# Encoder block on one core: stores issued later in SyncE's order, a head's steps drawn closer, the last low part ahead of evictions

## The chip, the core and the metric

The kernel runs on one core of a Trainium2 chip. Its engines work side by side, each through its own instructions in program order: TensorE (PE in the profile) multiplies, VectorE (DVE) and ScalarE (ACT) do elementwise work, SyncE (SP) issues nearly all DMA transfers, and GpSimd (POOL) issues the transfers that add to what is already in SBUF. An instruction that waits holds up everything behind it on its engine. The metric is device time in microseconds, as the median of repeated runs.

## What is computed

One encoder block with two branches, for 256 tokens of width 2048, in float32:

```python
xn = rms_norm(x, norm_pre_w[l])
z = xn @ w_in[l]
u_lru, g_lru, q, k, v, g_attn, m_lru, m_attn = jnp.split(z, split_at, axis=-1)
u = centred_depthwise_conv(u_lru, conv_w[l], conv_b[l])
h = rg_lru(u, ..., False) + rg_lru(u, ..., True)
y_a = h.astype(x.dtype) * jax.nn.silu(g_lru)
q = partial_rope(q.reshape(bsz, s, N_HEADS, HEAD_DIM), cos, sin)
k = partial_rope(k.reshape(bsz, s, N_KV_HEADS, HEAD_DIM), cos, sin)
y_b = windowed_gqa(q, k, v, attn_sink[l]) * jax.nn.silu(g_attn)
merged = (jax.nn.sigmoid(m_lru) * (y_a @ w_proj_a[l])
          + jax.nn.sigmoid(m_attn) * (y_b @ w_proj_b[l]))
x = x + rms_norm(merged @ w_out[l], norm_post_w[l])
```

There are 16 heads of width 128 in 4 groups; `w_in` has 13312 columns, the other three matrices 2048.

## The kernel before

**Two parts of each number.** Products are made with operands of a rounded type (fp32r). To keep float32 precision each operand is split into a high part (a cast, on ACT) and a low part (the rest, a subtraction on DVE), and three products are added: high by high, high by low and low by high. `lag_parts` (L120) issues such a cast at once and the subtraction one half step later.

**Steps and half steps.** The weights come in 182 loads of 1 MB. Each is a step: the load into one of three raw buffers, the cast into `wh` by `ahead` (L974), the subtraction into `wl` by `low` (L966), and the products with it. A step has two half steps, hs = 2i and 2i + 1. In the loop at the end of `body` (L991 to L1009), at half step 2i SP is given the load of step i + 3; then whatever has been put down for this half step is issued in the order in which it was put down; then, on even half steps, the cast of step i + 2; at last the products of the half step on PE. `at(hs, fn)` (L138) puts work down for a half step, `soon(fn, d)` (L147) for d half steps after the present one, and `early(hs, fn)` (L144) ahead of all other work of a half step. So half steps set each engine's order; when things run is up to the semaphores. A half step on PE is twelve wide products, or six in the saving scheme below.

**Steps that save products.** Some blocks are multiplied two by two with seven products instead of eight (`add_seven`, L587). Its weights are sums of blocks: a step of this kind adds its load to weights that are already in a "chain" buffer, by an accumulating DMA that POOL issues once the low part of the step before it in the chain is done. Its left sides are differences of activations (`sums`, L652), also split into parts.

**What goes to DRAM and back.** SBUF has 29 large buffers (`unit`). What isn't needed for long is stored and taken back later: the parts of four differences (xee1 to xee4, high and low), the sigmoids of the merge gates (tm0 to tm2, sm2 and sm3), and the gated output of the LRU branch in four pieces (ya0 to ya3). `put_away` (L124) issues such a store on SP, 0.5 MB each. A store on SP waits for the engine that makes its data, and the loads behind it wait with it. Merge gates and differences are stored four half steps after they are complete (L561, L670), ya two half steps after the gating that completes it: `lru_pair` (L444) gates 20 half steps after its base b, and L871 puts the store at b + 22.

**A head.** `head` (L753) puts the steps of one attention head down behind its base: `scores` (PE), `expo` (DVE: scale, mask, maximum), `powers` (ACT: exponential and sum), `normalise` (DVE and ACT: `p` times the reciprocal), `flip` (PE: transposes of `p` into `pt`), `p_parts` (ACT: `ph`, and one half step later DVE: `pl`), `values` (PE: product with v into `o`), `gate_out` (DVE: `o` times the gate). Heads start three half steps apart. There is one buffer for `ph` and one for `pl`, so a head's `ph` can be written only after the `values` of the head before.

**The end.** The last steps multiply by `w_out`; `take_o` (L928) evicts each block: squares and their sum on ACT, times the norm's weight on DVE. The last step is made for the first 128 tokens and then for the others, so that the first half's output can be finished beside the second half's products.

Of the kernel before, what the change touches and what calls it, by code (L numbers as in the profile page):

```python
# [27 lines left out]
EPS = 1e-6  # L28
UNITS = 29
CHAIN = 2  # L30
DECAY = 10
SPIN = 10
G = 1
LRU0 = 14
LRU_PACE = 22
# [47 lines left out]
def body(ctx, tc, x, xT, wall, wlru, pvec, npost, ident_d, mask_d, rope_d, out):  # L83
    nc = tc.nc
    const = ctx.enter_context(tc.tile_pool(name="const", bufs=1))
    units = ctx.enter_context(tc.tile_pool(name="units", bufs=UNITS))
    chain = ctx.enter_context(tc.tile_pool(name="chain", bufs=CHAIN))
    ring = ctx.enter_context(tc.tile_pool(name="ring", bufs=3))
# [5 lines left out]
    def unit(name, dt=F32, shape=(P, 4, S)):  # L94
        return units.tile(list(shape), dt, tag="u", name=name)

    def bank(name, shape=(P, 2, S)):
        return psum.tile(list(shape), F32, tag="bg", name=name, bufs=4)
# [4 lines left out]
    def half_unit(name, tag, dt=F32, bufs=2):  # L103
        return small.tile([P, 2, S], dt, tag=tag, name=name, bufs=bufs)
# [5 lines left out]
    def tiny(name, n=2):  # L110
        return small.tile([P, n], F32, tag="tiny", name=name, bufs=24)
# [8 lines left out]
    def lag_parts(h, l, src):  # L120
        nc.scalar.copy(h, src)  # L121
        soon(lambda: nc.vector.tensor_tensor(l, src, h.bitcast(F32), ALU.subtract))

    def put_away(name, t):  # L124
        d = away.tile(list(t.shape), F32, tag=name, name=f"{name}_away")
        nc.sync.dma_start(d, t.bitcast(F32))
        return d
# [7 lines left out]
    steps, due = [], {}  # L135
    now = [0]

    def at(hs, fn):  # L138
        assert hs >= now[0], (hs, now[0])
        due.setdefault(hs, []).append(fn)  # L140
# [6 lines left out]
    def soon(fn, d=1):  # L147
        at(now[0] + d, fn)
# [8 lines left out]
    def parts_tiles(i):  # L157
        highs[i], lows[i] = (ring.tile([P, 2048], F32R, tag=f"w{s}", name=f"w{s}{i}", bufs=3) for s in "hl")
# [18 lines left out]
    def pieces(i):  # L177
        if isinstance(raws[i], list):
            return [(slice(h * 1024, (h + 1) * 1024), t) for h, t in enumerate(raws[i])]
        return [(slice(0, 2048), raws[i])]  # L180
# [7 lines left out]
    def mm3(ps, wh, wl, xh, xl, start, stop):  # L188
        nc.tensor.matmul(ps, wh, xh, start=start, stop=False)
        nc.tensor.matmul(ps, wh, xl, start=False, stop=False)  # L190
        nc.tensor.matmul(ps, wl, xh, start=False, stop=stop)  # L191
# [232 lines left out]
    for i, fn in enumerate([  # L424
# [12 lines left out]
    ]):  # L437
        at(DECAY + i // 2, fn)


    sgl, sga = [], []
    ya, yb = [None] * 8, [None] * 8
# [109 lines left out]
    def gate_take(units_of, c, t, ps, scale=1.0):  # L552
        if c not in units_of:
            units_of[c] = unit(f"mg{c}", F32, (P, 2, 512))
        nc.scalar.activation(units_of[c][:, t], ps, AF.Sigmoid, scale=scale)
        if c in ((0, 1) if units_of is sm else (3,)):
            return
        name = "sm" if units_of is sm else "tm"
        written[name, c] = written.get((name, c), 0) + 1
        if written[name, c] == 2:  # L560
            soon(lambda: gone.update({(name, c): put_away(f"{name}{c}", units_of.pop(c))}), 4)  # L561

    gone, written = {}, {}

# [87 lines left out]
    def sums(name, y, keep=None):  # L652


        fm = lambda r, c, n: y[2 * c + n][:, :, r * P:(r + 1) * P]
        eight = lambda u: u.rearrange("p a (b c) -> p (a b) c", c=P)
        e, out = {}, {}

        def less(d, a, b):
            e[d] = e[b] if isinstance(b, str) else eight(unit(f"{name}{d}"))  # L660
            for n in range(2):
                f = [e[o][:, 4 * n:4 * n + 4] if isinstance(o, str) else fm(*o, n) for o in (a, b)]
                nc.vector.tensor_tensor(e[d][:, 4 * n:4 * n + 4], *f, ALU.subtract)

        def split_of(d):
            h, l = (unit(f"{name}{d}{s}", F32R, (P, 8, P)) for s in "hl")
            lag_parts(h, l, e[d])
            out[d] = (h, l)
            if keep is not None:
                soon(lambda: keep.update({d: [put_away(f"{name}{d}{s}", a) for a, s in ((h, "h"), (l, "l"))]}), 4)  # L670

        def when(hs, gap=2):
            for (d, a, b), n in zip((("e1", (1, 0), (1, 1)), ("e2", (0, 0), "e1"), ("e4", (0, 1), "e2"), ("e3", (1, 0), (0, 0))), hs):
                at(n, lambda d=d, a=a, b=b: less(d, a, b))
                at(n + gap, lambda d=d: split_of(d))
            at(hs[2] + 4, lambda: [e.pop(d) for d in ("e1", "e2", "e4")])
            at(hs[3] + 4, lambda: e.pop("e3"))

        return out, when
# [73 lines left out]
    def head(hd, qh, ql, b):  # L753
        g, j = hd // 4, hd % 4
        sk = pv[:, PV_SINK + hd:PV_SINK + hd + 1]
        ts = [slice(t * P, (t + 1) * P) for t in range(2)]
        v = {}

        def scores():
            v["sc"] = bank(f"sc{hd}")  # L760
            for t in range(2):
                mm3(v["sc"][:, t], qh[:, j, ts[t]], ql[:, j, ts[t]], kv["kh"][:, g], kv["kl"][:, g], True, True)

        def expo():
            p = v["p"] = half_unit(f"p{hd}", "p")
            sc = v.pop("sc")
            m, nm, es = tiny(f"m{hd}"), tiny(f"nm{hd}"), tiny(f"es{hd}")
            dn = v["dn"] = tiny(f"dn{hd}")
            for t in range(2):
                nc.vector.tensor_tensor_reduce(p[:, t], sc[:, t], mask[:, t], P ** -0.5, sk, ALU.add, ALU.max, m[:, t:t + 1])  # L770
            nc.vector.tensor_scalar(nm, m, -1.0, None, ALU.mult)
            v["nm"], v["es"] = nm, es

        def powers():
            p, nm, es, dn = v["p"], v["nm"], v["es"], v["dn"]
            for t in range(2):
                nc.scalar.activation(p[:, t], p[:, t], AF.Exp, bias=nm[:, t:t + 1], accum_out=dn[:, t:t + 1])
            nc.scalar.activation(es, nm, AF.Exp, bias=sk)

        def normalise():  # L780
            dn, rd = v["dn"], tiny(f"rd{hd}")
            nc.vector.tensor_tensor(dn, dn, v["es"], ALU.add)
            nc.vector.reciprocal(rd, dn)  # L783
            for t in range(2):
                nc.scalar.activation(v["p"][:, t], v["p"][:, t], AF.Copy, scale=rd[:, t:t + 1])  # L785

        def flip():
            v["pt"] = bank(f"pt{hd}")
            for kt in range(2):
                for t in range(2):  # L790
                    nc.tensor.transpose(v["pt"][:, kt, ts[t]], v["p"][:, t, ts[kt]], ident)

        def p_parts():
            v["h"] = half_unit(f"ph{hd}", "ph", F32R, 1)
            v["l"] = half_unit(f"pl{hd}", "pl", F32R, 1)
            lag_parts(v["h"], v["l"], v.pop("pt"))

        def values():
            v["o"] = bank(f"o{hd}")
            ks = slice(g * P, (g + 1) * P)  # L800
            for kt in range(2):
                mm3(v["o"][:, 0], kv["vh"][:, kt, ks], kv["vl"][:, kt, ks], v["h"][:, kt], v["l"][:, kt], kt == 0, kt == 1)

        def gate_out():
            y = sga[g][:, j]
            nc.vector.tensor_tensor(y, v["o"][:, 0], y, ALU.mult)
            v.clear()

        for d, fn in ((0, scores), (1, expo), (2, powers), (3, normalise), (6, flip), (7, p_parts), (10, values), (11, gate_out)):
            at(b + d, fn)  # L810

    ended = []
# [1 line left out]
    def heads(g):  # L814
        def then(h, l):
            b = max(now[0] + HEAD0, ended[-1] if ended else 0)
            for j in range(4):
                head(4 * g + j, h, l, b + HEADS_PACE * j)
            ended.append(b + 4 * HEADS_PACE)
        return then  # L820
# [47 lines left out]
        return pairs, when, chunk  # L868

    for c in range(4):  # L870
        at(LRU0 + LRU_PACE * (2 * c + 1) + 22, lambda c=c: gone.update({("ya", c): put_away(f"ya{c}", sgl[c])}))  # L871
    for i in range(4):
        plain += add_heads(f"q{i}", Q0 + i * 512, heads(i))
    plain += add_rows("ml3_", "w_in", ML0 + 3 * 512, xn, gate_evac(tm, 3))
# [91 lines left out]
    def low(i):  # L966
        for sl, t in pieces(i):
            nc.vector.tensor_tensor(lows[i][:, sl], t, highs[i][:, sl].bitcast(F32), ALU.subtract)  # L968
        if i in grow:
            n = grow[i]  # L970
            raws[n] = raws[i]
            nc.gpsimd.dma_start(raws[n], wall[rows_of[steps[n][0]]], accum_op=ALU.add)  # L972

    def ahead(i):  # L974
        if i < len(steps):
            parts_tiles(i)
            for sl, t in pieces(i):
                nc.scalar.copy(highs[i][:, sl], t)  # L978
            soon(lambda: low(i))

    tail = {}
    for i, (row, _, key) in enumerate(steps):
# [95 lines left out]
```

## Time and profile before

| what | value |
|---|---|
| median of 3 runs | 889.18 us (889.05 to 891.41) |
| the profiled execution | 895.12 us |
| its span | 893.3 us |
| granted TensorE clock, mean | 0.997 |
| DMA | 227.74 MB, mean 255 GB/s |
| stores to DRAM that the change moves | 17 of 0.5 MB |

The profile is of one execution. A row of the order of time has the start in us, the duration, the engine, the line in the kernel, the operation, output<-inputs and how many were merged; in brackets stands how long the engine idled before it and what ended that. A row of who waited for whom has the waiting engine, the one waited for, the total in us, the number of waits and the longest. A row of stretches has, behind its bounds, the busy time of PE, PE's weight loads, DVE, ACT and POOL, the granted clock as a share of full speed, the share of the DMA engines that was busy, and GB/s. `raw`, `chain`, `wh` and `wl` are the weights as loaded and their two parts. Numbers behind a name are left out in the rows, so that which step or head a row belongs to follows from its place in the engine's order.

### The profile page before, as it was taken

Reading aid. Unit: us, or ns where it says so; the run is one execution under the profiler, and the core shown is the slowest. Engines: PE = TensorE matmul, PEld = TensorE weight load, DVE = VectorE, ACT = ScalarE, POOL = GpSimd, SP = SyncE. Lnnn points to the kernel's source line nnn. Section 1 sums busy time; section 2 is a strip of 40 time slices with the busy share of each in tenths; the row PEclk is TensorE's granted clock in tenths of the full one; section 3 lists DMA queues with packets and bytes.
Section 4 is the critical chain, followed back from the end, with each engine's and each line's share of the span. In section 5 each row is a group of like instructions: output and inputs, shape, how many; then the busy total and the mean of one; then the engine's idle time right before and its main releaser. Section 6 shows DMA issues by size and latency. Waiting matters only on the chain.

```text
span 893.3 us, 11502 instructions
## 1 busy us (share of the span) xinstructions
PE 878.9 (98%) x4518; PEld 751.3 (84%) x4518; DVE 688.1 (77%) x740; ACT 622.0 (70%) x737; POOL 37.2 (4%) x49
## 2 busy tenths in 40 slices
PE   9999999999999999998999999999999999999996
PEld 9888888888888888886888888887888888888885
DVE  5987976979878695957968667777897767758786
ACT  6977659787777878748695766678966554546653
POOL 0000000000000000100000000000000000100000
PEclk9999999999999999999999999999999999999999
DMA  8756678878979887798699879836866986998893
GB/s 320 277 182 216 234 302 205 324 296 248 275 184 338 230 346 288 204 290 211 255 264 350 294 205 257 231 146 248 208 251 236 272 240 195 318 288 323 223 276 149
DMA packets 38934, 227.74 MB, mean 255 GB/s; under 512 B 4320, under 2 KB 5216, under 8 KB 16224
## 3 DMA queue, kind: packets, MB, share of 16 engines
q1 hardware_dynamic: 32400, 184.43, 54.9%
q0 software_dynamic: 6048, 41.95, 24.3%
q8 instruction: 35, 0.57, 0.2%
q10 hardware_dynamic: 432, 0.63, 0.2%
q14 instruction: 19, 0.16, 0.1%
HBM read 215.98 MB, written 11.01 MB: 254 GB/s over the span
## 4 chain that ended last, share of the span: by engine, by line
PE 83%; ACT 6%; DVE 5%; DMA 4%; issue 1%; SPq 0%; DVEq 0%; ACTq 0%
PE u L208 5%; PE ga L208 5%; PE gl L208 5%; DMA raw<-wall_dram 3%; DVE wl L968 3%; PE gl L210 3%; PE ga L210 3%; PE u L210 3%; PE q__4412 L239 2%; PE pa__5458 L239 2%; PE q__4814 L239 2%; PE v__622 L239 2%; PE ml L239 2%; PE pa__5824 L239 2%; PE q__3915 L239 2%; PE o__6841 L239 2%
## 5 line engine op out<-in xcount | busy, mean ns | idle before, releaser
L968 DVE TENSOR_TENSOR wl<-raw,wh 128x2048 fp32r<-128x2048 f32 x118 | 269.5, 2287 | 75.2 <-ACT wh L978 75.0
L978 ACT CAST wh<-raw 128x2048 fp32r<-128x2048 f32 x118 | 224.9, 1911 | 74.3 <-DMA raw<-wall_dram 23.8
L968 DVE TENSOR_TENSOR wl<-chain,wh 128x2048 fp32r<-128x2048 f32 x56 | 128.0, 2288 | 37.4 <-ACT wh L978 37.4
L978 ACT CAST wh<-chain 128x2048 fp32r<-128x2048 f32 x56 | 107.0, 1913 | 40.1 <-PE pb__6243 L239 7.4
L972 POOL DMA_DIRECT2D chain<-wall_dram x38 | 33.3, 876 | 781.2 <-DVE wl L968 625.8
L208 PE MATMUL ga<-xn,wh 128*128 128x512 f32 x256 | 62.8, 390 | 0.0
L208 PE MATMUL gl<-xn,wh 128*128 128x512 f32 x256 | 62.6, 390 | 0.0
L208 PEld LDWEIGHTS gl<-xn,wh 128*128 128x128 f32 x256 | 47.7, 188 | 9.1
L208 PEld LDWEIGHTS ga<-xn,wh 128*128 128x128 f32 x256 | 47.7, 188 | 9.1
L208 PE MATMUL u<-xn,wh 128*128 128x512 f32 x192 | 47.6, 391 | 0.0
L208 PEld LDWEIGHTS u<-xn,wh 128*128 128x128 f32 x192 | 35.5, 188 | 6.5
L210 PEld LDWEIGHTS ga<-xn,wl 128*128 128x128 f32 x256 | 32.8, 191 | 1.3
L210 PEld LDWEIGHTS gl<-xn,wl 128*128 128x128 f32 x256 | 32.8, 191 | 1.3
L210 PE MATMUL gl<-xn,wl 128*128 128x256 f32 x256 | 33.2, 283 | 0.0
L210 PE MATMUL ga<-xn,wl 128*128 128x256 f32 x256 | 33.2, 283 | 0.0
L210 PEld LDWEIGHTS u<-xn,wl 128*128 128x128 f32 x192 | 24.6, 191 | 1.0
L210 PE MATMUL u<-xn,wl 128*128 128x256 f32 x192 | 24.9, 283 | 0.0
L785 ACT ACTIVATE p<-p,rd 128x256 f32<-128x256 f32 x32 | 14.5, 503 | 14.6 <-DVE rd L783 14.6
L121 ACT CAST ph<-pt 128x512 fp32r<-128x512 f32 x16 | 9.3, 584 | 21.9 <-PE o L191 21.8
L469 DVE SCALAR_TENSOR_TENSOR up<-up,pv 128x255 f32<-128x255 f32 (+1 forms) x48 | 22.5, 481 | 1.1
L770 DVE CUSTOM_DVE_ANT_0 p<-sc,mask,pv 128x256 f32<-128x256 f32 x32 | 14.2, 479 | 7.5 <-PE sc L191 7.4
L398 PE MATMUL u_ps<-xs,wh 128*128 128x256 f32 x128 | 19.0, 291 | 0.5 <-ACT wh L114 0.5
(525 smaller groups left out, 1942.1 us busy)
## 6 DMA issues: line engine op xcount, KB each, us to landing
raw<-wall_dram SPq DMA_DIRECT2D x121, 1024.0 KB, 6.3
chain<-wall_dram POOLq DMA_DIRECT2D x38, 1024.0 KB, 9.3
chain<-wall_dram SPq DMA_DIRECT2D x18, 1024.0 KB, 6.1
lraw<-wlru_dram SPq DMA_DIRECT2D x8, 512.0 KB, 6.0
raw<-wall_dram SPq DMA_DIRECT2D x4, 512.0 KB, 7.3
ya_away<-sg SPq DMA_DIRECT2D x4, 512.0 KB, 6.8
yb<-ya_away SPq DMA_DIRECT2D x4, 512.0 KB, 9.2
pair<-wall_dram SPq DMA_DIRECT2D x4, 512.0 KB, 12.2
```

The source lines that it names most:

```text
L121: nc.scalar.copy(h, src)
L208: nc.tensor.matmul(ps, wh[:, sl], a, start=k == 0, stop=k == KT - 1)
L210: nc.tensor.matmul(ps[:, 1], wl[:, sl], a[:, 0], start=False, stop=False)
L239: nc.tensor.matmul(got[t], a[:, m], w[:, j * 512:(j + 1) * 512], start=k == 0 and m == 0 and not low, stop=low and k == KT - 1)
L398: nc.tensor.matmul(ups[b // 2][:, b % 2, 0], w[:, sl], a[:, m], start=k == 0 and n == 0, stop=k == KT - 1 and n == 2)
L469: nc.vector.scalar_tensor_tensor(u[:, a:b], up[:, a + tap - 2:b + tap - 2], cw[:, tap:tap + 1], u[:, a:b], ALU.mult, ALU.add)
L770: nc.vector.tensor_tensor_reduce(p[:, t], sc[:, t], mask[:, t], P ** -0.5, sk, ALU.add, ALU.max, m[:, t:t + 1])
L785: nc.scalar.activation(v["p"][:, t], v["p"][:, t], AF.Copy, scale=rd[:, t:t + 1])
L968: nc.vector.tensor_tensor(lows[i][:, sl], t, highs[i][:, sl].bitcast(F32), ALU.subtract)
L972: nc.gpsimd.dma_start(raws[n], wall[rows_of[steps[n][0]]], accum_op=ALU.add)
L978: nc.scalar.copy(highs[i][:, sl], t)
```

## The change

The constant AWAY is 8, where the two delays of stores were 4. The store of ya goes from b + 22 to b + 27. In a head the flip and what follows comes one or two half steps earlier. The low part of the last step is put ahead of the other work of its half step; for all other steps `at` does what `soon` did.

```diff
+AWAY = 8
...
-            soon(lambda: gone.update({(name, c): put_away(f"{name}{c}", units_of.pop(c))}), 4)
+            soon(lambda: gone.update({(name, c): put_away(f"{name}{c}", units_of.pop(c))}), AWAY)
...
-                soon(lambda: keep.update({d: [put_away(f"{name}{d}{s}", a) for a, s in ((h, "h"), (l, "l"))]}), 4)
+                soon(lambda: keep.update({d: [put_away(f"{name}{d}{s}", a) for a, s in ((h, "h"), (l, "l"))]}), AWAY)
...
-        for d, fn in ((0, scores), (1, expo), (2, powers), (3, normalise), (6, flip), (7, p_parts), (10, values), (11, gate_out)):
+        for d, fn in ((0, scores), (1, expo), (2, powers), (3, normalise), (5, flip), (6, p_parts), (8, values), (9, gate_out)):
             at(b + d, fn)
...
-        at(LRU0 + LRU_PACE * (2 * c + 1) + 22, lambda c=c: gone.update({("ya", c): put_away(f"ya{c}", sgl[c])}))
+        at(LRU0 + LRU_PACE * (2 * c + 1) + 23 + AWAY // 2, lambda c=c: gone.update({("ya", c): put_away(f"ya{c}", sgl[c])}))
...
-            soon(lambda: low(i))
+            (early if i == len(steps) - 1 else at)(now[0] + 1, lambda: low(i))
```

## The prediction

> **What bounds the kernel now.** I read the page's first part, then who waited for whom on the tensor engine (PE), and then the instructions in order of time around each of its waits.
>
> ```profile
> span 893.3 us, 11502 instructions
> PE 878.9 (98%) x4518; PEld 751.3 (84%) x4518; DVE 688.1 (77%) x740; ACT 622.0 (70%) x737; POOL 37.2 (4%) x49
> ```
>
> PE is the bound: its work is fixed and no edit touches it. So the change can win only the holes in PE's stream, and what follows PE's last product. A hole is larger than the idle time shown, because the end of a matmul is modelled; I measure it from start to start. The pace without waits comes from the last products:
>
> ```profile
> 882.82 1.98 PE L239 MATMUL o<-wh,ms 128*128 128x512 f32 x8
> 884.63 1.07 PE L239 MATMUL o<-wl,ms 128*128 128x512 f32 x4
> ```
>
> Eight products start 884.63 - 882.82 = 1.81 us apart, 0.227 each. The holes:
>
> ```profile
> 407.05 1.07 PE L603 MATMUL mbn<-wl,e0e2h 128*128 128x512 f32 x4
> 412.04 0.50 PE L603 MATMUL mbn<-wh,e0e2h 128*128 128x512 f32 x1 [3.93 <-ACT wh L978]
> ...
> 416.69 0.50 PE L239 MATMUL k__3696<-wh,xn 128*128 128x512 f32 x1
> ...
> 412.00:417.00 5.00, 4.93 (x13) 3.62 (x14) 3.32 (x3) 4.96 (x5) 0.87 (x1) 0.66 0.64 107
> ...
> 436.31 1.52 PE L603 MATMUL mbq<-wh,xn 128*128 128x512 f32 x6
> 438.01 1.20 PE L603 MATMUL mbq<-wl,xn 128*128 128x512 f32 x4 [0.18 <-DVE wl L968]
> 439.04 0.62 PE L239 MATMUL k__3696<-wh,xn 128*128 128x512 f32 x2
> ```
>
> **Hole 1.** Four products from 407.05 should end their turn at 407.96; the next starts at 412.04: 4.08 us. Then 12 products take 416.69 - 412.04 = 4.65 where 2.72 is normal: 1.93 more, because the granted clock (the stretch 412 to 417, last column but two) fell to 0.66. At 436.31 ten products take 2.73 where 2.27 is normal: 0.46, ACT and DVE still late. Sum 6.47.
>
> The rule on this gate (Trainium skill, "TensorE: Matmul & The Clock Gate", section "HAM oscillation — how this bites in real kernels") is that PE gaps over some 3.4 us are to be avoided, since the clock halves behind them. The trace agrees: 4.08 us cost 1.93 more. By the rule a hole that shrinks below that loses the second part at once.
>
> **Hole 2** (a head's values) and **hole 3** (the last weights):
>
> ```profile
> 613.74 1.54 PE L239 MATMUL ml__5137<-wl,xn 128*128 128x512 f32 x6
> 616.02 0.35 PE L189 MATMUL o<-ph,vh 128*128 128x256 f32 x1 [0.73 <-ACT wh L978]
> ...
> 617.22 0.28 PE L189 MATMUL sc<-kh,q3h 128*128 128x256 f32 x1
> 617.34 0.28 PE L190 MATMUL sc<-kl,q3h 128*128 128x256 f32 x1
> ...
> 876.83 1.98 PE L239 MATMUL o<-wh,ms 128*128 128x512 f32 x8
> 879.04 1.20 PE L239 MATMUL o<-wl,ms 128*128 128x512 f32 x4 [0.24 <-DVE wl L968]
> 880.08 2.00 PE L239 MATMUL o<-wh,ms 128*128 128x512 f32 x8
> ```
>
> Six wide products and six narrow ones (617.34 - 617.22 = 0.12 apart) should take 2.08; 617.22 - 613.74 = 3.48: 1.40 lost. Twelve products from 876.83 should take 2.72 and take 3.25: 0.53. All holes: 6.47 + 1.40 + 0.53 = 8.40 us.
>
> **The stores.** Hole 1 begins 33 us before PE stops: ACT idles for a load, and that load was issued in a crowd.
>
> ```profile
> 396.91 1.91 ACT L978 CAST wh<-raw 128x2048 fp32r<-128x2048 f32 x1 [10.17 <-DMA raw<-wall_dram]
> ...
> 374.33 22.48 DMA raw<-wall_dram
> ...
> 370.81 0.33 SPq L126 DMA_DIRECT2D ya_away<-sg  x1
> 371.23 1.61 SPq L175 DMA_DIRECT2D raw<-wall_dram  x2
> ...
> SPq L126 <- DVE sg L520: 20.1, 1, 20.1
> ...
> 356.00:371.00 15.00, 15.00 (x83) 13.04 (x82) 13.09 (x14) 12.89 (x12) 1.75 (x2) 1.00 0.58 107
> 371.00:397.00 26.00, 26.00 (x150) 22.92 (x149) 17.05 (x16) 10.60 (x13) 1.74 (x2) 1.00 1.01 316
> ...
> 353.93 2.29 DVE L968 TENSOR_TENSOR wl<-raw,wh 128x2048 fp32r<-128x2048 f32 x1 [1.06 <-ACT wh L978]
> ...
> 367.17 2.28 DVE L968 TENSOR_TENSOR wl<-raw,wh 128x2048 fp32r<-128x2048 f32 x1
> ```
>
> SP stands 20.1 us, from 350.7, at the store of ya2 (half step 146), which waits for the gating of an LRU pair. Behind it are the loads of steps 77 and 78, two of 0.5 MB (e0e2) and the load of step 79, the one ACT waits for. Before 371 the DMA engines move 107 GB/s, afterwards they are full (share 1.01, 316 GB/s).
>
> The edit puts ya2 at half step 151, behind loads 77 and 78. No instruction is added, and no queue but SP's is involved. Each load still needs one of three raw buffers: 77 the one freed by the low part that ends at 353.93 + 2.29 = 356.2, 78 the one freed at 367.17 + 2.28 = 369.5. So a new wait takes the place of much of the old one: SP stands until 369.5 for load 78, and ya2 follows at 370.8 as before. What is gained is that load 77, 1.05 MB, moves from 371.2 to 356.2, into the slack stretch. At least 1.05 MB / 316 GB/s = 3.3 us come off the landing of load 79. More is likely: the late part of that stretch is shared with POOL's accumulating loads, and 3.7 MB on SP's queue instead of 4.7 (each piece 1.05 or 0.52) could pass before they start. I take a landing near ACT's need (396.91 - 10.17 = 386.7). Bounds: with 3.3 us off, 0.8 of hole 1's 4.08 stays, and the clock part goes (behind hole 2, 1.40 us long, the pace is undisturbed): 3.3 + 1.93 = 5.2 gained; with all off, 6.47. I take **6.47**.
>
> A rule of the Trainium skill ("DMA: Bandwidth & Descriptors", section "Queues, rings and completion order") speaks against it: an engine takes turns between its queues, so the early load 77 would slow POOL's load beside it. The trace leaves room for both: 107 GB/s before 371 against 316 behind it. At worst POOL's load lands load 77's own 3.3 us later, and of the 6.47 the low bound's 5.2 is left.
>
> The other 16 stores (8 of the differences' parts, 3 tm, 2 sm, 3 ya) move the same way past two or three loads. PE has no hole near them, so I cost them at nothing; PE covers them, and without that cover each would give back its own SP wait. Their buffers are held four or five half steps longer; counted in the code, the fullest such place (half step 60) would need all 29 units, which fits. Nothing waits there that the trace shows.
>
> **The heads.** Flip moves from 6 to 5 half steps behind a head's scores, its parts from 7 to 6, values from 10 to 8, gating from 11 to 9. No work is added. What goes is ACT's wait: it may write the single ph buffer only after the values of the head before, and these stood in the same half step (10 = 3 + 7). Now they stand one ahead (8 against 3 + 6).
>
> ```profile
> ACT ph L121 <- PE o L191: 21.8, 9, 5.2
> ...
> 609.19 2.89 PE L239 MATMUL ml__5137<-wh,xn 128*128 128x512 f32 x12
> ...
> 596.62 0.90 ACT L785 ACTIVATE p<-p,rd 128x256 f32<-128x256 f32 x2
> 602.70 0.59 ACT L121 CAST ph<-pt 128x512 fp32r<-128x512 f32 x1 [5.18 <-PE o L191]
> ...
> 610.50 0.91 ACT L785 ACTIVATE p<-p,rd 128x256 f32<-128x256 f32 x2 [3.29 <-DVE rd L783]
> ...
> 613.24 2.29 DVE L968 TENSOR_TENSOR wl<-raw,wh 128x2048 fp32r<-128x2048 f32 x1 [2.25 <-ACT wh L978]
> ...
> 615.79 0.68 DVE L122 TENSOR_TENSOR pl<-pt,ph 128x512 fp32r<-128x512 f32 x1
> ```
>
> Hole 2 is the end of this chain: ACT held 5.18 us at 597.5, DVE late behind it, then ACT behind DVE, and pl of head 10 done at 616.5, when PE wanted it at 615.1. What is new is a shorter lead: PE takes pl one half step after DVE is given it, not two. For head 10 that means 609.2 (half step 240). With ph of head 9 written at 597.5, what is behind it comes about 5.2 us earlier: 616.5 - 5.2 = 611.3; and pl's new place is ahead of the low part at 613.24, so that it waits neither for that (2.29) nor for ACT's cast before it (2.25): near 606.8, an estimate from these rows, 2.4 us in hand. Gone through in the same way, the tightest head is the last, 15: its pl would follow the low part at 659.01 + 2.28, so end near 661.9, and PE wants it near 661.6. Value taken: **1.40** gained. Other end: the relief fails and the short lead bites (the slow rival).
>
> ```profile
> 659.01 2.28 DVE L968 TENSOR_TENSOR wl<-raw,wh 128x2048 fp32r<-128x2048 f32 x1
> ...
> 660.28 2.03 PE L603 MATMUL pap<-wh,pay 128*128 128x512 f32 x8
> ...
> 873.40 1.92 ACT L978 CAST wh<-raw 128x2048 fp32r<-128x2048 f32 x1 [0.81 <-PE oq L603]
> ...
> 874.83 0.68 DVE L626 TENSOR_TENSOR ot<-oq,ot 128x512 f32<-128x512 f32 x1
> 876.69 2.29 DVE L968 TENSOR_TENSOR wl<-raw,wh 128x2048 fp32r<-128x2048 f32 x1
> 878.90 0.68 DVE L640 TENSOR_TENSOR ot<-oq,ot 128x512 f32<-128x512 f32 x1
> ```
>
> (Half step 259 starts with the seventh product from 660.28: 661.6.)
>
> **The last low part** starts now at 876.69, behind evictions. Placed ahead of those of its half step it starts when ACT's cast (875.32) and DVE's subtraction (875.51) are done and ends at 877.8; PE wants it at 876.83 + 1.81 = 878.64. So **0.53** is won. The evictions overtaken, about 1.2 us, run from 877.8 to 879.0, just where the next one stands now (878.90), so nothing behind them is later. The 7.6 us after PE's end stay.
>
> **The sum.** The profiled execution took 895.12, 1.82 more than its span. 895.12 - 8.40 = 886.7. But the median shown is 889.18, 5.9 below the profiled time, so ordinary executions seem to carry only some 2.5 us of the holes: about holes 2 and 3 and little of hole 1. PE's floor is the same, so the forecast is **886.7**, 0.28% under the median. About 0.3% is what a measurement can tell from no change, here 886.5 and 891.8.
>
> **Rivals.**
> - *A: forecast*, holes closed on PE's floor of 886.7, 885.7 to 888.0. Chance 0.50.
> - *B: the profiled execution is slower by something else*, and ordinary ones carry hole 1 too. With all of it 889.18 - 8.40 = 880.8; without its clock part, 889.18 - (8.40 - 1.93) = 882.7; with half of it, 889.18 - 1.93 - 3.2 = 884.0 (holes 2 and 3 make 1.93 too). For it: the runs shown go from 889.05 to 891.41, about one clock part apart. Against: PE's stream in the trace has no other loss to name. 0.27.
> - *C, slower: the short lead bites.* If ACT keeps its lateness, ph of head 10 comes behind the scaling that ends at 610.50 + 0.91 = 611.4, and its pl (0.59 + 0.68 later) at 612.7, against 609.2: a hole of 3.5 us. Head 15 adds its 0.3, and a clock loss as behind hole 1 up to 1.93: 886.7 + 5.7 = 892.4. It decides from 5.1 us of new holes, so only if the clock falls too. Against it: the lateness comes from the very wait that goes. 0.13. By the gate's rule named above a hole of 3.5 just reaches the length at which the clock falls.
> - *D: the stores do nothing*, since load 78 holds SP as long and hole 1 hardly exists in ordinary runs, and small new waits in the heads eat the rest: 888.5 to 889.5. 0.10.
>
> Faster by over 0.3%: 0.4 of A (its part below 886.5) and B, 0.20 + 0.27 = 0.47. Within: 0.30 + 0.10 = 0.40. Slower: 0.13. Range 882.5 to 891.0: it leaves out the lower part of B (0.1) and most of C (0.1).
>
> **What would show it.** Right: load 77 issued near 356, before ya2; load 79 landing by 387 to 393; no PE gap near 408 and the granted clock at 1.00 there; ACT's wait for values at ph near nothing; PE steady from 876.83 to its end. Wrong: PE waits at the heads' values for pl, a wait of the flip for ACT's scaling, hole 1 still there, or a time under 885, which would mean that ordinary runs held more of hole 1 than I take.

## The result and the profile after

| kernel | median us | executions | ratio to before |
|---|---|---|---|
| before, the runs beside the changed kernel | 891.56 (889.05 to 895.03) | 9 | 1 |
| changed | 886.82 (885.74 to 889.24) | 9 | 0.9943 [0.9922, 0.9963] |

The time is the one forecast, 886.7. The gain is twice the 0.28% that stood beside it: nine executions of the kernel before have a median of 891.56, where the three that were shown had 889.18.

The changed kernel's profiled execution took 886.14. Its page, first and fourth part:

```profile
PE 874.2 (99%) x4518; PEld 750.1 (85%) x4518; DVE 687.7 (78%) x740; ACT 623.4 (70%) x737; POOL 37.3 (4%) x49
...
PE 98%; DMA 1%; DVE 0%; ACT 0%; issue 0%; SPq 0%; DVEq 0%
```

The fourth part of the kernel before:

```profile
PE 83%; ACT 6%; DVE 5%; DMA 4%; issue 1%; SPq 0%; DVEq 0%; ACTq 0%
```

The same products, and PE is now nearly the whole chain that ended last. Who waited for whom, the changed kernel, all that PE waited for, then ACT at `ph`, and SP at the stores of ya (waiting engine, the one waited for, total us, times, longest):

```profile
PE u_ps L399 <- ACT wh L115: 1.2, 2, 0.8
PE spin L279 <- POOL eps L274: 1.0, 1, 1.0
PE u_ps L399 <- DVE wh L115: 0.3, 1, 0.3
...
ACT ph L122 <- PE pt L792: 4.4, 3, 2.6
...
SPq L127 <- DVE sg L521: 1.9, 2, 1.0
```

No wait of PE behind the start-up is left. ACT's 21.8 us for the values of the head before are gone, with a smaller wait for the flip in their place, and SP's longest stand at a store of ya fell from 20.1 to 1.0. Lines have moved down by one against the kernel before.

Where the time went, the changed kernel in order of time, around hole 1 and at the last weights (columns as before):

```profile
355.92 13.57 SPq L176 DMA_DIRECT2D raw<-wall_dram  x2
370.48 0.33 SPq L127 DMA_DIRECT2D ya_away<-sg  x1
...
372.69 0.33 SPq L176 DMA_DIRECT2D raw<-wall_dram  x1
...
386.28 1.92 ACT L979 CAST wh<-raw 128x2048 fp32r<-128x2048 f32 x1
...
406.71 1.07 PE L604 MATMUL mbn<-wl,e0e2h 128*128 128x512 f32 x4
407.62 0.39 PE L604 MATMUL mbn<-wh,e0e2h 128*128 128x512 f32 x1
...
410.34 3.79 PE L240 MATMUL k__3696<-wh,xn 128*128 128x512 f32 x16
...
868.39 1.98 PE L240 MATMUL o<-wh,ms 128*128 128x512 f32 x8
870.20 1.07 PE L240 MATMUL o<-wl,ms 128*128 128x512 f32 x4
871.11 1.98 PE L240 MATMUL o<-wh,ms 128*128 128x512 f32 x8
```

and two stretches of it:

```profile
356.00:371.00 15.00, 15.00 (x82) 12.96 (x81) 13.20 (x13) 12.90 (x11) 1.75 (x2) 1.00 0.81 185
412.00:417.00 5.00, 5.00 (x24) 4.14 (x23) 5.00 (x7) 2.43 (x2) 0.00 (x0) 1.00 0.98 303
```

Load 77 is issued at 355.92, ahead of ya2; the stretch before 371 moves 185 GB/s instead of 107; ACT casts load 79 at 386.28 without a wait, where it had waited 10.17 us until 396.91; the products that stood still at 407.96 go on, and the granted clock is 1.00. The lead over the trace of before, read at products with the same place in the order, grows at three places. It is 407.05 - 406.71 = 0.34 ahead of hole 1, 416.69 - 410.34 = 6.35 behind its first part and 446.11 - 439.00 = 7.11 behind both (half step 176). It is 876.83 - 868.39 = 8.44 behind the heads, and the last product starts 885.31 - 876.32 = 8.99 earlier. At the last weights 1.81 and 0.91 between the rows are the steady pace.

### The profile page after: what moved, and what is told of

It is laid out like the page before. It is cut to its first block, busy times and chain, and to the rows that moved or that the text cites. A ratio compares the mean times of both kernels' runs of the same rounds, so it can differ in the third digit from the quotient of the medians.

```text
span 884.4 us, 11518 instructions
## 1 busy us (share of the span) xinstructions
PE 874.2 (99%) x4518; PEld 750.1 (85%) x4518; DVE 687.7 (78%) x740; ACT 623.4 (70%) x737; POOL 37.3 (4%) x49
## 3 DMA queue, kind: packets, MB, share of 16 engines
q1 hardware_dynamic: 32400, 184.43, 55.7%
q0 software_dynamic: 6048, 41.95, 24.6%
## 4 chain that ended last, share of the span: by engine, by line
PE 98%; DMA 1%; DVE 0%; ACT 0%; issue 0%; SPq 0%; DVEq 0%
PE ga L209 7%; PE gl L209 7%; PE u L209 5%; PE ga L211 3%; PE gl L211 3%; PE u L211 3%; PE ml__5148 L240 2%; PE q__4817 L240 2%; PE pa__5466 L240 2%; PE q__4415 L240 2%; PE q__4184 L240 2%; PE v__622 L240 2%; PE ml L240 2%; PE q__3915 L240 2%; PE k__3696 L240 2%; PE o__6841 L240 2%
## 5 line engine op out<-in xcount | busy, mean ns | idle before, releaser
L211 PEld LDWEIGHTS u<-xn,wl 128*128 128x128 f32 x192 | 24.6, 191 | 1.0
L778 ACT ACTIVATE p<-p,nm 128x256 f32<-128x256 f32 x32 | 16.1, 505 | 5.1 <-DVE nm L772 5.1
## 6 DMA issues: line engine op xcount, KB each, us to landing
pair<-wall_dram SPq DMA_DIRECT2D x4, 512.0 KB, 12.4
```

The lines of the kernel that those rows point to most:

```text
L211: nc.tensor.matmul(ps[:, 1], wl[:, sl], a[:, 0], start=False, stop=False)
```

## The experiments

What the kernels with a ratio gave; "before" in them is the old kernel on the same chip, whose medians were 892.0, 893.1 and 891.9 in the three sets (888.8 to 897.3 in all).

| kernel | median us | ratio to before |
|---|---|---|
| stores alone | 889.53 (887.8 to 890.5) | 0.9963 [0.9943, 0.9984] |
| heads alone | 890.03 (886.1 to 894.2) | 0.9984 [0.9961, 1.0007] |
| ya at b + 23, alone | 890.72 (888.75 to 896.36) | 1.0001 [0.9977, 1.0025] |
| ya at b + 24, alone | 888.05 (887.61 to 889.47) | 0.9959 [0.9941, 0.9978] |
| ya at b + 24, heads, low part | 887.03 (885.74 to 887.36) | 0.9925 [0.9897, 0.9954] |
| the changed kernel again | 886.86 (885.86 to 890.27) | 0.9938 [0.9914, 0.9962] |
| the changed kernel, ya back at b + 22 | 889.02 (887.17 to 893.52) | 0.9960 [0.9937, 0.9983] |
| old kernel, e0e2 taken back earlier | 888.13 (887.39 to 888.91) | 0.9951 [0.9928, 0.9973] |
| changed kernel, e0e2 taken back earlier | 886.37 (885.92 to 887.17) | 0.9922 [0.9895, 0.9950] |

### The change in two halves

The kernel before with the stores' edits alone (`4` to `8` twice, ya `+ 22` to `+ 27`), and with the head's line alone.

> The kernel before with the 17 stores moved as in the change, heads and last low part as before. My theory (hole 1 comes from load 77 standing behind the ya2 store): no PE gap near 408, load 77 issued near 356, holes 2 (1.4 us) and 3 (0.5 us) still there; about 1.9 us above the changed kernel, near 888.7 where the kernel before gives 891.6, a ratio near 0.997. Rival (hole 1 goes because the shorter heads or the whole set of edits shift the work): a gap near 408 stays and the ratio is 1.000.

> The kernel before with the four head offsets of the change alone. My theory: hole 1 as before (load 77 issued near 371, a gap near 408 in most executions), hole 2 gone, ACT's wait for values at ph near nothing; about 1.4 us below the kernel before, a ratio near 0.998. Rival (the heads carry the gain): hole 1 gone, 2 us or more below the stores alone.

The stores alone bring 0.37% and close hole 1; holes 2 and 3 stand in its trace, 1.4 and 0.7 us by the measure of the prediction. The heads alone close hole 2 and leave hole 1, though a smaller one, 3.39 us against the changed kernel's trace where the kernel before had 6.78; their 0.16% is what hole 2's 1.40 us are, but the interval takes in no change at all. In both, the holes that the other half should close are there, so the parts act apart.

### Which store, and by how much

```diff
-        at(LRU0 + LRU_PACE * (2 * c + 1) + 22, lambda c=c: gone.update({("ya", c): put_away(f"ya{c}", sgl[c])}))
+        at(LRU0 + LRU_PACE * (2 * c + 1) + 23, lambda c=c: gone.update({("ya", c): put_away(f"ya{c}", sgl[c])}))
```

and the same with `+ 24`; nothing else is changed.

> The kernel before with the four ya stores one half step later, b + 23 for b + 22, nothing else. ya2 then stands at half step 147, still ahead of load 77 (148). My theory: nothing changes, SP stands some 20 us at ya2, load 77 issued near 371, time as the kernel before. Rival (what counts is how late the store is): a small part of the gain, a twentieth to a fifth.

> The kernel before with the four ya stores two half steps later, b + 24, nothing else. ya2 then stands at half step 148, just behind load 77. My theory: this one place is all of hole 1: load 77 issued near 356, no PE gap near 408, time some 1.9 us above the changed kernel, near 888.7, as with all stores moved. Rival (later is better, or the other 13 stores count): a gap of 1 us or more near 408, and a time between the kernel before and the stores alone.

SP's order of time, first ya at b + 23:

```profile
371.89 0.33 SPq L126 DMA_DIRECT2D ya_away<-sg  x1
372.31 1.54 SPq L175 DMA_DIRECT2D raw<-wall_dram  x2
...
393.37 1.90 ACT L978 CAST wh<-raw 128x2048 fp32r<-128x2048 f32 x1 [5.54 <-DMA raw<-wall_dram]
```

then ya at b + 24:

```profile
355.83 0.33 SPq L175 DMA_DIRECT2D raw<-wall_dram  x1
370.40 0.33 SPq L126 DMA_DIRECT2D ya_away<-sg  x1
370.83 0.44 SPq L175 DMA_DIRECT2D raw<-wall_dram  x1
...
386.22 1.92 ACT L978 CAST wh<-raw 128x2048 fp32r<-128x2048 f32 x1
```

A half step later shows no gain, 1.0001 (0.9977 to 1.0025), for loads are issued on even half steps and ya2 still stands ahead of load 77. One more half step carries it past that one load, and ACT no longer waits. That is all of the stores' gain: 0.9959 against 0.9963 with all 17 stores moved by four or five. Load 78, issued at 370.83 where all stores moved have it at 369.16, does no harm. The profiled executions of all kernels part in the same way: load 79 landed at 392.5 to 396.8 in the four with load 77 behind ya2, and at 384.0 to 391.3 in the eight with it ahead (the two kernels below with e0e2 taken back earlier aside).

### The other stores

The kernel before with ya at b + 24, the heads and the low part, so that the 13 other stores stand where they stood; and the changed kernel with ya put back (`+ 23 + AWAY // 2` to `+ 22`). The changed kernel itself ran beside them.

> The ya stores at b + 24, heads and last low part as in the change, the other 13 stores where they were before. My theory: all three holes closed with four stores moved by two half steps, the 13 others are worth nothing; time as the changed kernel, near 886.5, or 0.5 to 1 us under it if the later stores crowd some load. Rival (the other stores matter): 1 us or more over the changed kernel.

> The changed kernel with the four ya stores back at b + 22; the other 13 stores, heads and last low part as changed. My theory: load 77 again near 371 and hole 1 back, as large as the landing of load 79 makes it; times spread over some 6 us as before, median 2 to 5 us over the changed kernel. Rival (the other stores help hole 1): as the changed kernel within 1 us.

> The changed kernel again, beside the others of this call: 886 to 887.5, no hole after the start.

Without the 13 other moves the time is 887.03, and 886.86 with them: nothing that these runs can tell. (Its trace has a hole of some 0.5 us at 868, where ACT had waited 3.54 us for a late chain load, and the trace of the changed kernel with e0e2 taken back earlier, below, one of 0.4; the changed kernel's own two traces have none there.) With ya back, load 77 is issued at 372.4 again, ACT waits 4.7 us, and the median is 2.2 us up. The changed kernel's second profiled execution holds a surprise. Its order of time, SP and ACT:

```profile
372.42 0.33 SPq L176 DMA_DIRECT2D raw<-wall_dram  x1
...
390.47 1.91 ACT L979 CAST wh<-raw 128x2048 fp32r<-128x2048 f32 x1 [4.31 <-DMA raw<-wall_dram]
```

Every issue lies within 0.3 us of the first execution's, yet load 79 landed 18.0 us after its issue and not 11.3, ACT waited 4.31, and PE took 0.9 us longer from 405 to 439 than in the first, most of it, measured from start to start, 0.3 at 409.9 and 0.45 at 431.0. So the change makes hole 1 small; it doesn't close it in every execution.

### What crowds the load

If it is the bunch of transfers behind 370 that makes load 79 late, and not SP's stand as such, then something else taken out of the bunch should do as well. `sums_back` puts down the two loads of e0e2 (0.5 MB each) nine half steps ahead of their use; here fifteen, in the old kernel and in the changed one.

```diff
-            at(2 * steps.index(woven[14 * (r + 1) + n]) - 9, lambda d=d: back(d))
+            at(2 * steps.index(woven[14 * (r + 1) + n]) - (15 if r == 0 and d == "e2" else 9), lambda d=d: back(d))
```

> The kernel before with the two loads of e0e2 at half step 145, ahead of the ya2 store, and nothing else. ya2 still holds SP for 20 us. My theory (hole 1 is the crowd, and 1 MB out of it does the same whichever MB it is): load 77 near 371 as before, load 79 lands near 385 to 391 instead of 392 to 397, hole 1 at most 1 us, time near 888 to 889 as with ya at b + 24. Rival (the store's wait itself is what costs): hole 1 as before, ratio 1.000.

> The changed kernel with the two loads of e0e2 (0.5 MB each) given to SP at half step 145 instead of 151, so near 350 instead of 371. My theory (what delays load 79 is all that is issued between 370 and 373): load 79 lands some 3 us earlier again, by 381 to 387, ACT doesn't wait for it, and the slower runs of the changed kernel (888 to 890) go; median 0 to 0.7 us under the changed kernel's 886.8, spread under 2 us. Rival (the landing varies by itself): same median and spread as the changed kernel, 885.7 to 890.3.

SP's order of time, the old kernel with this edit:

```profile
349.79 0.38 SPq L131 DMA_DIRECT2D e0e2h<-xee2h_away  x1
360.62 0.33 SPq L131 DMA_DIRECT2D e0e2l<-xee2l_away  x1
369.84 0.32 SPq L126 DMA_DIRECT2D ya_away<-sg  x1
370.21 2.16 SPq L175 DMA_DIRECT2D raw<-wall_dram  x3
```

SP still stands at ya2 until 369.84 and loads 77, 78 and 79 follow it in one go. But 1 MB less is in the bunch: load 79 lands after 15.8 us, ACT waits 2.2, and PE has no hole there. The median is 888.13, as good as ya's move by itself. So the bunch is the cause, and the stand costs only by what it bunches. Both together (886.37) are 0.5 below the changed kernel's 886.86; these came from different sets, and their ratios, 0.9922 and 0.9938, have intervals that overlap, so that it is better is not shown. The landing expected there, by 381 to 387, was missed: e0e2's second half goes out at 361.75, ahead of load 77 at 362.12, and load 79 landed at 388.4, 15.2 us after its issue, with no wait of ACT for it.

### Why the heads' edit closes hole 2

The prediction gave two reasons at once: ACT's wait for the values of the head before goes, and `pl` is put ahead of the low part. Three versions of the head's line in the changed kernel, each run once. The first keeps flip and parts as changed and puts the values one half step later, so that the wait of ACT comes back:

```diff
-        for d, fn in ((0, scores), (1, expo), (2, powers), (3, normalise), (5, flip), (6, p_parts), (8, values), (9, gate_out)):
+        for d, fn in ((0, scores), (1, expo), (2, powers), (3, normalise), (5, flip), (6, p_parts), (9, values), (10, gate_out)):
```

The second has `(6, flip), (7, p_parts), (9, values), (10, gate_out)`: flip and parts as in the kernel before, values one earlier, so that the wait is gone and the lead is as short as in the change. The third has `(4, flip), (5, p_parts), (7, values), (8, gate_out)`, all one earlier than the change.

> The changed kernel with values at 9 and gating at 10 half steps, flip and parts at 5 and 6 as changed. Values of a head then stand again in the half step in which the next head's ph is written (9 = 3 + 6). My theory of hole 2 (ACT held at ph by the values of the head before): ACT's waits for values at ph come back, some 15 to 22 us in all, and a gap at head 10's values of up to 1.5 us may come back too. Rival (the earlier flip and gating alone do it): those waits stay near nothing.

> The changed kernel with flip and parts where they were before (6 and 7), values at 9 and gating at 10: the next head's ph is free one half step before it is written, and pl has one half step as lead. Theory W (hole 2 comes from ACT's wait for values): that wait is near nothing, pl of head 10 ready before its values, no gap there. Rival P (what closes hole 2 is that ph and pl come a half step earlier against the run of short half steps): a gap of 0.5 us or more at head 10 or 11, because pl is late.

> The changed kernel with flip at 4, parts at 5, values at 7 and gating at 8: one half step less again. It tests the slow rival's mechanism, a lead too short. In the changed kernel the flip follows the scaling by 0.9 us at heads 4 and 11 and pl is ready 0.0 to 0.9 us ahead of values at heads 6, 10, 12, 13, 15. With a half step (1.4 to 2.8 us) less, PE should wait at the flips of heads 3, 4 and 11 for ACT's scaling, 0.5 to 2 us each, 1.5 to 5 us in all, time 888 to 891. Rival (ACT and DVE run ahead by as much): no wait of PE, time as the changed kernel.

The first, who waited for whom:

```profile
ACT ph L122 <- PE o L192: 25.0, 11, 5.4
```

and DVE, then PE, in order of time at head 10:

```profile
603.31 0.68 DVE L123 TENSOR_TENSOR pl<-pt,ph 128x512 fp32r<-128x512 f32 x1
605.32 2.29 DVE L969 TENSOR_TENSOR wl<-raw,wh 128x2048 fp32r<-128x2048 f32 x1 [1.32 <-ACT wh L979]
...
607.26 0.28 PE L190 MATMUL o<-ph,vh 128*128 128x256 f32 x1
607.37 0.28 PE L191 MATMUL o<-pl,vh 128*128 128x256 f32 x1
```

The wait is back in full, 25.0 us, and PE has no hole there: `pl` is done at 603.99, 3.4 us before its product. The second, who waited for whom:

```profile
PE o L191 <- DVE pl L123: 1.3, 1, 1.3
```

and the same place, DVE, then PE:

```profile
604.00 2.29 DVE L969 TENSOR_TENSOR wl<-raw,wh 128x2048 fp32r<-128x2048 f32 x1 [1.92 <-ACT wh L979]
606.21 0.68 DVE L123 TENSOR_TENSOR pl<-pt,ph 128x512 fp32r<-128x512 f32 x1
...
605.39 0.28 PE L190 MATMUL o<-ph,vh 128*128 128x256 f32 x1
606.95 0.39 PE L191 MATMUL o<-pl,vh 128*128 128x256 f32 x1 [1.28 <-DVE pl L123]
```

The wait is gone, and hole 2 is there. So ACT's wait for values going is neither needed, by the first version, nor enough, by the second. That it is worth nothing is not shown: the second version's lead is a half step shorter than that of the kernel before. From the start of half step 240 (602.67 here, 609.19 before) its `pl` ends after 4.22 us where that took 7.28, 3.1 sooner, and its values are wanted 3.2 sooner, so that the shorter lead may have used up what the wait gave. What decides at head 10, with the change's lead, is `pl`'s place in DVE's order: put down for half step 239 it stands ahead of that half step's low part; for 240 it stands behind it, and with it behind DVE's wait for ACT's cast (1.92) and the subtraction (2.29).

The third opens new holes. Who waited for whom:

```profile
PE o L191 <- DVE pl L123: 2.4, 2, 1.9
```

and DVE, then PE, in order of time at head 10:

```profile
600.92 2.28 DVE L969 TENSOR_TENSOR wl<-raw,wh 128x2048 fp32r<-128x2048 f32 x1
...
603.39 0.67 DVE L123 TENSOR_TENSOR pl<-pt,ph 128x512 fp32r<-128x512 f32 x1
...
601.96 0.28 PE L190 MATMUL o<-ph,vh 128*128 128x256 f32 x1
604.12 0.39 PE L191 MATMUL o<-pl,vh 128*128 128x256 f32 x1 [1.88 <-DVE pl L123]
604.34 0.28 PE L192 MATMUL o<-ph,vl 128*128 128x256 f32 x1
604.46 0.28 PE L190 MATMUL o<-ph,vh 128*128 128x256 f32 x1
```

The step from 601.96 to 604.12 is 2.16 where 0.12 is normal: 2.04 us at head 10, 0.7 at head 2, 0.3 at a flip, and 3.3 in all against the changed kernel's trace. Here too `pl`, put down for half step 238, stands behind a low part, the one of 237. Its single time was 889.39, beside 886.8 for the change. The flip moved up from half step 5 to 4 had been expected to stall at three heads, and only one shows it. The two other single times, 888.2 and 888.11, hold remains of hole 1 and hole 2 respectively, and settle nothing by themselves.

## Why the prediction was right or wrong

**Time and floor: right.** PE's floor of 886.7 came from adding up the holes of one trace; the changed kernel gave 886.82 and 886.86. That it agrees to 0.1 is luck: the two profiled executions are 895.12 - 886.14 = 8.98 apart where 8.40 was forecast, and the median of the changed kernel lies 0.68 above its profiled execution, so two misses cancel.

**Hole 1: right in mechanism and near in size.** Load 77 was forecast at 356.2 and ahead of ya2, and came at 355.9; load 78 held SP until 369.5, as said, and ya2 followed at 370.5. The gain between the two traces there is 446.11 - 439.00 = 7.11 at half step 176, less the 0.34 ahead of it: 6.77, where 6.47 was forecast. The landing was set near 386.7 with 3.3 us off as the worse bound. It came at 384.0 in one execution and at 390.4 in the other, both within the stated 387 to 393 or earlier, and the later one costs PE 0.9 us. That the other 13 stores are worth nothing was right. The weakness of the step is the word "closed" where the trace could only have said "small".

**The base: wrong.** The step that failed is "ordinary executions seem to carry only some 2.5 us of the holes: about holes 2 and 3 and little of hole 1", and with it rival D. It was read from the median of three executions. With ya's store moved past one load, and nothing else, the kernel gains 0.9959 [0.9941, 0.9978], so ordinary executions of the old kernel do carry hole 1: 0.41% of 892, 3.7 us, at the median, and more in the profiled execution of 895.12, which is in the upper part of what was seen (888.8 to 897.3). Against the changed kernel's trace that execution lost 6.78 us at hole 1; the traces of heads alone, ya at b + 23 and ya back at b + 22, where load 77 also stands behind ya2, lost 3.39, 2.15 and 1.31. Rival B had hole 1 in ordinary executions, but on a base of 889.18 and so a floor under 884; the base was higher, and the floor stood. The kernels whose trace shows no hole there (stores alone, ya at b + 24 with and without the rest, e0e2 earlier in both) spread over 1.3 to 2.7 us, the changed kernel over 3.5 and 4.4, the old one over 7.5 to 8.5 in each of the three sets, with more executions. With ten to twelve executions each, as three of the first group have, ya at b + 23, heads alone and ya back spread over 7.6, 8.1 and 6.4: the spread goes with the bunch.

**Hole 2: the size right, one of the two reasons over-sized.** 1.40 was forecast; at half step 262 the two traces differ by 669.25 - 660.82 = 8.43, and at 240 by 609.19 - 602.16 = 7.03: 1.40. The step "what is behind it comes about 5.2 us earlier" failed. The wait went, but ACT's cast of q3 in the same stretch then waited for PE, and DVE for ACT. The changed kernel in order of time, ACT, DVE and PE:

```profile
592.97 0.59 ACT L122 CAST q3h<-q3p 128x512 fp32r<-128x512 f32 x1 [2.94 <-PE q3p L740]
...
597.49 0.69 DVE L123 TENSOR_TENSOR q3l<-q3p,q3h 128x512 fp32r<-128x512 f32 x1 [3.70 <-ACT q3h L122]
...
601.49 0.68 DVE L123 TENSOR_TENSOR pl<-pt,ph 128x512 fp32r<-128x512 f32 x1
603.82 2.29 DVE L969 TENSOR_TENSOR wl<-raw,wh 128x2048 fp32r<-128x2048 f32 x1 [1.65 <-ACT wh L979]
...
602.16 0.28 PE L190 MATMUL o<-ph,vh 128*128 128x256 f32 x1
602.28 0.33 PE L191 MATMUL o<-pl,vh 128*128 128x256 f32 x1
```

`pl` ends at 602.17 and its product starts at 602.28: nothing in hand, where 2.4 was forecast. The low part behind it starts at 603.82 where it started at 613.24; less the 7.03 that PE was ahead by then it is 2.4 us earlier, not 5.2. The reason that held is the other one, the place ahead of the low part (603.82), and the version with the change's lead, the old place and no wait shows that without it the hole returns. Head 15, named as the tightest, has 0.75 in hand; head 10, with 0.11, is the tightest.

**Rival C: not as told.** The short lead doesn't bite at 8 = 6 + 2 behind the scores; with 7 = 5 + 2 it costs 3.3 us. But the rival had ACT keep its lateness and `ph` come late; in the version with 7 `ph` of head 10 is written at 598.05, ahead of need, and `pl` is late because it stands behind a low part. No clock loss stood behind its longest hole.

**The last low part: right.** 0.53 was forecast; the lead grows from 8.44 to 8.99, 0.55. The low part, the changed kernel on DVE in order of time:

```profile
867.44 2.28 DVE L969 TENSOR_TENSOR wl<-raw,wh 128x2048 fp32r<-128x2048 f32 x1
869.64 0.69 DVE L937 TENSOR_TENSOR yw<-ot,np 128x512 f32<-128x512 f32 x1
```

It ends at 869.72, and PE wants it at 870.20: 0.5 in hand, 0.8 had been worked out. This part wasn't tried alone.

**The queues' turns.** The cost that was weighed is not settled. Of POOL's two loads beside the early load 77 the first took 7.8 us from issue to landing, 8.0 before. The second took 9.3 in the changed kernel's first profiled execution and 12.9 in its other one. Over the eight traces with load 77 ahead it took 9.2 to 13.3, and 9.6 to 11.4 over the four with load 77 behind ya2. So an early load 77 doesn't always slow it, and may in some executions. The rule of the Trainium skill ("DMA: Bandwidth & Descriptors", section "Queues, rings and completion order") is neither borne out nor refuted by this.

A difference of 0.34 us between the traces by half step 24 was not predicted; it is in the start-up, and its cause was not tried.

## What to carry to other kernels

A store that waits in an in-order queue costs by the transfers that it bunches up behind it; look for the load that comes last out of the bunch, and take one transfer out of it, which here needed one place in the order for one store (the edit moves four; PE has a hole behind one), or two small loads asked for earlier. Read a lead between engines together with the order inside the step: at head 10 the place ahead of or behind a 2.3 us instruction made or closed the hole, while 25.0 us of another engine's waits, in the version that had them, cost PE nothing. Here a single trace gave the floor well (add up the holes), and the base badly: before setting a gain against a median, see how far executions of the old kernel spread.

## What the runs showed of the hardware

**The same load, issued at the same time, lands at different times.** In five traces whose kernels are the same in this stretch (the changed one twice, stores alone, values at 9, and the third version of the heads) loads 77 and 79 are issued within 0.3 us of each other's times, and load 79 (1 MB) took 11.3, 18.0, 12.4, 18.6 and 12.6 us to land. In a sixth (the second version of the heads), issued 0.5 us later, it took 15.3. POOL's second accumulating load, issued near 364.3, goes with it: 9.3, 12.9, 9.4, 13.3, 9.7 and, in the sixth, 10.6 us. What makes both slow in an execution is open. The two longest are of one set on one chip; the kernel with ya back, of the same set, had the shortest landing of the four with the bunch (17.0), so the chip alone doesn't explain them.

**Accumulating loads are dear.** The page's third part, the changed kernel (queue, kind, packets, MB, share of the engines' time); q0 carries POOL's accumulating loads:

```profile
q1 hardware_dynamic: 32400, 184.43, 55.7%
q0 software_dynamic: 6048, 41.95, 24.6%
```

24.6 / 41.95 against 55.7 / 184.43 is 1.94 times the engine time for a byte. Two of them are issued in the stretch before 371 and two between 371 and 397. That adding makes them dear, and not that POOL issues them, is not shown, for all that POOL issues add.

**The clock and the length of a hole.** Behind the old kernel's 4.08 us the granted clock fell to 0.66 and cost 1.93 more. Behind holes of 1.27 us (heads alone), 1.43 (the second version of the heads) and 2.04 (the third) it stayed at 1.00, and from the second product on the pace was the normal 0.12 or 0.23. That agrees with the Trainium skill ("TensorE: Matmul & The Clock Gate", section "HAM oscillation — how this bites in real kernels"), which puts the length to avoid at some 3.4 us; no run here has a hole between 2.04 and 4.08.
